# Moving the tiles that TensorE reads to multiples of 256 bytes in a hybrid encoder layer

## The chip, the core and the metric

The kernel runs on one core of a Trainium2 chip. The metric is the device time of one execution in microseconds, the median of several runs. An SBUF address is meant per partition: a tile of 128 x 512 float32 takes 2,048 bytes in each of 128 partitions.

## The reference, cut to what matters

One encoder layer is applied with the same weights to two inputs, a prompt of 1,024 tokens and a sample of 512, both 1,024 wide, in float32.

```python
proj = rmsnorm(x, g_attn) @ w_in                 # 1024 x 5120: qa ka va qb kb vb, two gates
a = dilated_mixture(qa, ka, va) @ w_a_out        # 12 heads in 3 dilation groups
bo = window_gqa(qb, kb, vb, sink) @ w_b_out      # 8 heads, window of +-128, sink per head
g_a, g_b = split(sigmoid(gates + b_gate))
x = x + (g_a * a + g_b * bo) @ w_o
u = dwconv(rmsnorm(x, g_ffn) @ w_up)             # 1024 x 5632, width 3
x = x + (gelu(u_gate) * u_val) @ w_down          # 2816 x 1024
y = rmsnorm(x, g_final)
```

## The kernel before, in words

**Precision.** Every float32 operand of a product is split into two float32r tiles, a rounded `hi` and the rest `lo`, and a product is three matmuls: hi by hi, hi by lo, lo by hi (`mm3`, lines 144 to 149; `accumulate`, lines 793 to 805; `product`, line 932; `down`, lines 1056 to 1058). Weights are loaded by SP's queue into `raw`, rounded by ScalarE (line 138) and their rests are taken by GpSimd or VectorE (line 141).

**The order of the work.** First the sample, then the prompt: norm and transposes, attention, merge (gates, branch projections, w_o), feed-forward. The sample's feed-forward (`ffn`) multiplies directly. In its loop the prompt's norm is done too (`norm_in`, line 206). The prompt's up-projection (`up_strassen`) makes seven products m1 to m7 per block of 128 columns in place of eight, each of 12 matmuls; m1, m2, m5, m6 have the moving operands b11, b21, t1, t2, which lie in the pool hp1024, and m4, m3, m7 have t4, b22, t3, which lie in hc1024. The order in the loop is m1, m2, m5, m6, then m4 and m3 of the block before, then m7. The prompt's `down` follows.

**Matmuls.** 7,944 matmuls have 512 moving columns. In `mm3` and `product` the moving operand is the activation and the stationary one (the weights of the array) a 128 x 128 piece of a weight tile; in the accumulations of lines 801 to 803 the moving operand is the weight tile and the stationary one the activation. The value projections (lines 289 to 291) have 256 moving columns of weights and the activations as stationary operand.

**Memory.** A pool is a stack entry: pools opened one after another lie one behind the other, some from the lower end of SBUF upwards (the default side), some from the upper end downwards. The sample's own pools lie at the lower end, except its inputs `xin` and small norm tiles `nsm`; the prompt's lie at the upper end, except the tiles of the Strassen weights and sums and hc. A tile's size is rounded up to 32 bytes. All tiles that matmuls read, but for two of the setup, are multiples of 512 bytes. So a pool of short tiles (`sm`, `ms`, `fsm`, `nsm`: 16 to 768 bytes each) shifts each pool that is opened behind it. A pool's first tile takes the lowest buffer, the next ones the others from the highest down. When a pool is closed, the next pool that is opened takes its place, and the first write of a tile waits for the last reader of the tiles that lay there (`reuse_waits="tile"`). The framework orders each engine's instructions itself, by priority and a model of times.

The lower end begins at byte 16,512, the upper end of the last pool is 229,344. At the lower end come the constants: `ident` (512 bytes), `eps`, `warm`, `sink`, `nsink` (32 each after rounding), `vecs` (832), so the next pool begins at 17,984, which is 70 x 256 + 64; 229,344 is 895 x 256 + 224. With the sizes of the pools this gives each pool's start modulo 256, which all its 512-byte pieces share:

| pools | start modulo 256 |
|---|---|
| raw, split (weights hi, lo); hp512 (the sample's activations); ptp512, qk512, vg512 (its attention); abp512, mg512, wop512 (its merge); wdp512 (its w_down); hc1024, rw1024 (Strassen operands and split weights, down's operands) | 64 |
| gvp512 (the sample's gated values, behind fsm512) | 192 |
| hp1024, ptp1024, qk1024, vg1024, abp1024, mg1024 (the prompt's) | 224 |
| xin512, xin1024 (behind nsm) | 96 |
| ident | 128 |

The pool mg1024 lies at 57,312 to 73,696, hp1024 at 163,808 to 229,344.

**The seam at the sample's feed-forward.** The last step of the merge (`accumulate`, lines 793 to 805) adds the blocks 6 and 7 of `merged` into x, token tile by token tile. Their operands lie in mg512, at 149,056 to 165,440: `mhi` in four buffers of 2,048 bytes, then `mlo`. Block 4 has the lowest buffer of mhi, block 7 the second, block 6 the third, block 5 the highest. The gate tiles mtp512 lie at 128,576 to 149,056. Then `begin_prompt` opens hp1024 and calls `begin_norm` (lines 1107 to 1109), which opens nsm1024 (4,224 bytes) and xin1024 (four tiles of 4,096 bytes, 143,200 to 159,584) from the upper end downwards; the sample's feed-forward takes its normalized tiles `xn` from xin1024. `rstd` (line 171 on) squares the x tiles on ScalarE into xn (line 175), takes a square root (line 176), and VectorE scales (line 190) before TensorE transposes (line 198).

**Constants.** `sink` is loaded by SP's queue (line 1139), negated on VectorE into `nsink` (line 1141) and used in `window_rows` (line 541) and, negated, in `window_unit`.

## Time and profile before

| | |
|---|---|
| median of 3 runs | 2,314.33 us (2,311.37 to 2,317.36) |
| profiled execution | 2,317.28 us, span 2,315.4 us |
| mean granted TensorE clock | 0.982 of full |
| TensorE busy | 2,207.3 us, 95% of the span |
| VectorE, ScalarE, GpSimd busy | 53%, 44%, 23% |
| DMA | 240.80 MB, mean 104 GB/s |

The span runs from the first to the last instruction of the program. A busy engine is one that has an instruction in flight; matmuls overlap, so the duration of one is longer than the distance to the next, and a stage in which TensorE is busy throughout can still become shorter if that distance does. L147 is line 147 of the kernel; `psg<-hhi,whi` names the tile that is written and the tiles that are read.

### The profile page before, as it was taken

What the parts mean: (1) busy time and instruction counts of PE and PEld (TensorE: products, weight loads), DVE (VectorE), ACT (ScalarE), POOL (GpSimd) and SP (SyncE); (2) the same over time, 40 slices, a digit from 0 to 9 for tenths busy, and PEclk for the clock granted to TensorE, in tenths of its full rate; (3) what the DMA queues carried; (4) which work ended last, traced back from release to release, by engine and by line L of the source; (5) the groups of instructions that cost most, each with busy time, mean ns of one, the idle gap of its engine ahead of it and who ended that gap; (6) DMA issues with size and microseconds to landing.
All of it is one profiled execution on the core that took longest, in us unless ns stands there. A gap on an engine that the chain in (4) does not pass through costs nothing.

```text
span 2315.4 us, 28400 instructions
## 1 busy us (share of the span) xinstructions
PE 2207.3 (95%) x10626; PEld 1820.2 (79%) x10626; DVE 1238.4 (53%) x2143; ACT 1015.8 (44%) x1868; POOL 542.3 (23%) x322
## 2 busy tenths in 40 slices
PE   6999899899999999999999999996899999999997
PEld 5887677688878788988787688885788888888886
DVE  4547533544465446465685534325867776763534
ACT  4646532533444336555575221114544444443332
POOL 2211254333333411100000432223332222200000
PEclk9999999999999999999999899998899999999999
DMA  5453442333333322413114711113122222254543
GB/s 159 141 167 113 146 153 85 110 94 98 100 124 94 100 78 60 129 58 110 51 49 120 217 44 50 44 35 118 37 83 86 79 81 82 78 200 150 173 152 112
DMA packets 247838, 240.80 MB, mean 104 GB/s; under 512 B 19792, under 2 KB 204832, under 8 KB 247700
## 3 DMA queue, kind: packets, MB, share of 16 engines
q1 hardware_dynamic: 247416, 238.89, 33.1%
q8 instruction: 83, 1.36, 0.2%
q14 instruction: 55, 0.45, 0.1%
q10 hardware_dynamic: 284, 0.11, 0.0%
HBM read 202.46 MB, written 42.79 MB: 106 GB/s over the span
## 4 chain that ended last, share of the span: by engine, by line
PE 78%; DVE 4%; ACT 2%; issue 2%; POOL 2%; DMA 1%; SPq 0%; DVEq 0%; ACTq 0%; POOLq 0%
PE psuA L932 10%; PE psuC L932 5%; PE pacc L803 4%; PE pacc L802 4%; PE pacc L801 4%; PE psg L147 3%; PE psg L149 3%; PE psg L148 3%; PE pacc L1058 3%; PE pacc L1056 3%; PE pacc L1057 3%; PE psu L147 3%; PE psu L149 3%; PE psu L148 3%; PE psuB L932 2%
## 5 line engine op out<-in xcount | busy, mean ns | idle before, releaser
L141 POOL TENSOR_TENSOR wlo<-raw,whi 128x1024 fp32r<-128x1024 f32 (+1 forms) x120 | 282.5, 2360 | 883.9 <-ACT whi L138 675.0
L138 ACT CAST whi<-raw 128x1024 fp32r<-128x1024 f32 (+1 forms) x178 | 182.1, 1029 | 385.8 <-PE pacc L803 137.1
L805 DVE TENSOR_TENSOR xacc<-xacc,pacc 128x512 f32<-128x512 f32 x236 | 160.5, 688 | 144.7 <-PE pacc L803 142.7
L147 PE MATMUL psg<-hhi,whi 128*128 128x512 f32 x384 | 152.0, 396 | 1.2 <-ACT frow L505 1.2
L141 DVE TENSOR_TENSOR wlo<-raw,whi 128x1024 fp32r<-128x1024 f32 (+1 forms) x58 | 74.4, 1282 | 147.2 <-ACT whi L138 124.6
L148 PE MATMUL psg<-hlo,whi 128*128 128x512 f32 x384 | 151.9, 395 | 0.0
L149 PE MATMUL psg<-hhi,wlo 128*128 128x512 f32 x384 | 151.7, 395 | 0.0
L147 PE MATMUL psu<-hhi,whi 128*128 128x512 f32 x352 | 137.5, 391 | 0.0
L149 PE MATMUL psu<-hhi,wlo 128*128 128x512 f32 x352 | 137.4, 391 | 0.0
L148 PE MATMUL psu<-hlo,whi 128*128 128x512 f32 x352 | 137.1, 390 | 0.0
L1057 PE MATMUL pacc<-rlo,rhi 128*128 128x512 f32 x352 | 137.1, 389 | 0.0
L1058 PE MATMUL pacc<-rhi,rlo 128*128 128x512 f32 x352 | 137.0, 389 | 0.0
L1056 PE MATMUL pacc<-rhi 128*128 128x512 f32 x352 | 137.0, 389 | 0.0
L939 DVE TENSOR_TENSOR rlo<-wraw,rhi 128x512 fp32r<-128x512 f32 x88 | 57.3, 689 | 133.2 <-ACT rhi L938 133.2
L968 POOL TENSOR_TENSOR rsum<-rraw 128x512 f32<-128x512 f32 x44 | 65.7, 1493 | 267.2 <-DMA rraw<-in_w_up_dram 251.2
L938 ACT CAST rhi<-wraw 128x512 fp32r<-128x512 f32 x88 | 50.5, 618 | 147.3 <-PE pacc L1058 137.9
L783 DVE TENSOR_TENSOR sg<-sg,psa 128x512 f32<-128x512 f32 x48 | 33.0, 687 | 153.2 <-PE psa L149 119.0
L938 ACT CAST rhi<-rsum 128x512 fp32r<-128x512 f32 x88 | 54.4, 622 | 117.7 <-PE psuC L932 71.2
L147 PE MATMUL psq<-hhi,whi 128*128 128x512 f32 x240 | 100.3, 418 | 1.1 <-DVE vb L341 0.6
L148 PE MATMUL psq<-hlo,whi 128*128 128x512 f32 x240 | 96.7, 403 | 0.0
L149 PE MATMUL psq<-hhi,wlo 128*128 128x512 f32 x240 | 96.2, 401 | 0.0
L399 DVE TENSOR_TENSOR ptlo<-pst,pthi 128x512 fp32r<-128x512 f32 (+1 forms) x128 | 82.7, 654 | 14.9 <-ACT pthi L398 13.4
(249 smaller groups left out, 6119.7 us busy)
## 6 DMA issues: line engine op xcount, KB each, us to landing
raw<-in_w_in_dram SPq DMA_DIRECT2D x80, 512.0 KB
raw<-in_w_up_dram SPq DMA_DIRECT2D x44, 512.0 KB
rraw<-in_w_up_dram SPq DMA_DIRECT2D x44, 512.0 KB
wraw<-in_w_down_dram SPq DMA_DIRECT2D x44, 512.0 KB
raw<-in_w_down_dram SPq DMA_DIRECT2D x22, 512.0 KB
gv<-y SPq DMA_DIRECT2D x22, 512.0 KB
graw<-gv SPq DMA_DIRECT2D x44, 256.0 KB
raw<-in_w_o_dram SPq DMA_DIRECT2D x16, 512.0 KB
```

The costliest lines, as they stand in the source:

```text
L138: nc.scalar.copy(out=hi[:, :n], in_=raw[:, :n])
L141: eng.tensor_tensor(out=lo[:, :n], in0=raw[:, :n], in1=hi[:, :n].bitcast(F32), op=ALU.subtract)
L147: mm(out, whi, r[0], start=start, stop=False)
L148: mm(out, whi, r[1], start=False, stop=False)
L149: mm(out, wlo, r[0], start=False, stop=stop)
L801: mm(p, a, whi[:, cols], start=i == 0, stop=False)
L805: nc.vector.tensor_tensor(out=x, in0=x, in1=p, op=ALU.add)
L932: mm(out, a[:, cols], b, start=start and j == 0 and n == 0, stop=j == 3 and n == 2, skip_group_check=True)
L938: nc.scalar.copy(out=hi, in_=src)
L1056: mm(p, a, whi, start=k == 0, stop=False)
L1057: mm(p, a, wlo, start=False, stop=False)
L1058: mm(p, b, whi, start=False, stop=k == FT - 1)
```

## The change

It changes where tiles lie, by three means. The short constants go into one tile `vecs` of 224 columns (896 bytes), and the separate `sink` goes: it is loaded into `nsink`, negated there, and `window_rows` subtracts it where it added `sink`. The constants then end at 17,920, which is 70 x 256. At the upper end a pool `top` with one tile of 224 bytes is opened first and never used, so the next pool ends at 229,120, which is 895 x 256. And pools of short tiles are opened behind those with tiles that TensorE reads: sm and ms last in `attention`, fsm behind gvp in `ffn`, nsm behind xin in `begin_norm`. All pools of the table then start at a multiple of 256, except `ident`, which stays where it is (at 128).

```diff
 window_rows
-                                in1=self.c["sink"][:, h].unsqueeze(1).to_broadcast([P, NT, 4]), op=ALU.add)
+                                in1=self.c["nsink"][:, h].unsqueeze(1).to_broadcast([P, NT, 4]), op=ALU.subtract)
 attention
         self.op = pool("ost", 4 if wide else 2)
-        self.sm = pool("sm", 2)
-        self.ms = pool("ms", 1)
         self.ptp = pool("ptp", 5 if wide else 4)
...
         self.vs = pool("vs", 2 if wide else 1)
+        self.sm = pool("sm", 2)
+        self.ms = pool("ms", 1)
 ffn
+        gvp = pool("gvp", 3)
         sm = pool("fsm", 2)
-        gvp = pool("gvp", 3)
 begin_norm
+        self.xin = self.pool(ctx, "xin", 4, side=side)
         self.nsm = self.pool(ctx, "nsm", 2, side=side)
-        self.xin = self.pool(ctx, "xin", 4, side=side)
 hybrid_encoder_kernel
-    c["eps"] = const.tile([P, 1], F32, name="eps")
+    vecs = const.tile([P, 224], F32, name="vecs")
+    top = ctx.enter_context(tc.tile_pool(name="top", bufs=1, side="right" if nc.default_side == "left" else "left"))
+    top.tile([P, 56], F32, name="top")
+    c["eps"], c["nsink"] = vecs[:, 208:209], vecs[:, 210:218]
     nc.gpsimd.memset(c["eps"], EPS)
-    warm = const.tile([P, 1], F32, name="warm")
-    nc.scalar.activation(out=warm, in_=c["eps"], func=AF.Sqrt)
+    nc.scalar.activation(out=vecs[:, 209:210], in_=c["eps"], func=AF.Sqrt)
     c["g_final"] = g_final
-    c["sink"] = const.tile([P, 8], F32, name="sink")
-    nc.sync.dma_start(c["sink"], bass.AP(tensor=sink.tensor, offset=sink.offset, ap=[[0, P], [1, 8]]))
-    c["nsink"] = const.tile([P, 8], F32, name="nsink")
-    nc.vector.tensor_scalar(out=c["nsink"], in0=c["sink"], scalar1=-1.0, scalar2=None, op0=ALU.mult)
-    vecs = const.tile([P, 208], F32, name="vecs")
+    nc.sync.dma_start(c["nsink"], bass.AP(tensor=sink.tensor, offset=sink.offset, ap=[[0, P], [1, 8]]))
+    nc.vector.tensor_scalar(out=c["nsink"], in0=c["nsink"], scalar1=-1.0, scalar2=None, op0=ALU.mult)
...
-        nc.vector.tensor_copy(out=vecs, in_=pv[:, 0:208])
+        nc.vector.tensor_copy(out=vecs[:, 0:208], in_=pv[:, 0:208])
```

## Rows read from the trace of the kernel before

**Rows 1.** The page, part 1: busy time, share of the span and instructions by engine.
```profile
PE 2207.3 (95%) x10626; PEld 1820.2 (79%) x10626; DVE 1238.4 (53%) x2143; ACT 1015.8 (44%) x1868; POOL 542.3 (23%) x322
```
**Rows 2.** Windows: the prompt's attention, merge, up- and down-projection; length, busy by engine, PEclk.
```profile
core 0: us, PE busy (x) PEld busy (x) DVE busy (x) ACT busy (x) POOL busy (x), PEclk, DMA share, GB/s
820.00:1248.00 428.00, 417.02 (x2539) 360.58 (x2538) 257.02 (x644) 252.31 (x614) 39.93 (x24) 0.99 0.24 75
1248.00:1597.00 349.00, 343.11 (x1443) 272.95 (x1441) 131.43 (x178) 76.58 (x103) 102.69 (x58) 0.98 0.32 90
1627.00:2066.00 439.00, 432.49 (x1858) 350.63 (x1857) 313.82 (x352) 219.69 (x328) 121.41 (x83) 0.99 0.26 86
2066.00:2303.00 237.00, 237.00 (x1047) 196.09 (x1046) 101.58 (x175) 82.30 (x147) 0.00 (x0) 1.00 0.45 151
```
**Rows 3.** Groups by line and shape, TensorE: busy us, mean ns of one, idle before.
```profile
L1056 PE MATMUL pacc<-rhi 128*128 128x512 f32 x352 | 137.0, 389 | 0.0
...
L932 PE MATMUL psuA<-b11hi,rhi 128*128 128x512 f32 x88 | 34.8, 396 | 0.0
...
L932 PE MATMUL psuA<-t3hi,rhi 128*128 128x512 f32 x88 | 34.3, 390 | 0.0
```
**Rows 4.** Timeline, TensorE: first and 48th matmul of a sample gate block (start us, us).
```profile
377.57 0.39 PE L147 MATMUL psg<-hhi,whi 128*128 128x512 f32 x1
...
388.22 0.39 PE L149 MATMUL psg<-hhi,wlo 128*128 128x512 f32 x1
```
**Rows 5.** Timeline, TensorE: first and 48th matmul of a prompt gate block.
```profile
1397.48 0.39 PE L147 MATMUL psg<-hhi,whi 128*128 128x512 f32 x1
...
1408.48 0.40 PE L149 MATMUL psg<-hhi,wlo 128*128 128x512 f32 x1
```
**Rows 6.** Timeline, TensorE, one Strassen round: first matmuls of m1, m4, m3, next m1.
```profile
1825.27 0.40 PE L932 MATMUL psuA<-b11hi,rhi 128*128 128x512 f32 x1
...
1836.51 0.39 PE L932 MATMUL psuA<-t4hi,rhi 128*128 128x512 f32 x1
...
1839.27 0.39 PE L932 MATMUL psuC<-b22hi,rhi 128*128 128x512 f32 x1
...
1844.71 0.40 PE L932 MATMUL psuA<-b11hi,rhi 128*128 128x512 f32 x1
```
**Rows 7.** Timeline, TensorE: first and 48th matmul, sample's down, then prompt's w_o accumulation.
```profile
638.66 0.40 PE L801 MATMUL pacc<-whi,ghi 128*128 128x512 f32 x1
...
649.58 0.40 PE L803 MATMUL pacc<-whi,glo 128*128 128x512 f32 x1
...
1428.39 0.40 PE L801 MATMUL pacc<-whi,mhi 128*128 128x512 f32 x1
...
1439.37 0.39 PE L803 MATMUL pacc<-whi,mlo 128*128 128x512 f32 x1
```
**Rows 8.** Timeline, TensorE, value projections: sample (42 matmuls), prompt (192), first and last.
```profile
92.57 0.28 PE L289 MATMUL psv<-whi,hhi 128*128 128x256 f32 x1
...
97.49 0.28 PE L291 MATMUL psv<-whi,hlo 128*128 128x256 f32 x1
...
820.70 0.39 PE L289 MATMUL psv<-whi,hhi 128*128 128x256 f32 x1
...
843.72 0.28 PE L291 MATMUL psv<-whi,hlo 128*128 128x256 f32 x1
```
**Rows 9.** Tile vb: sample 234 to 252, prompt 1140 to 1248 us; duration ns min/median/max.
```profile
L409 PE MATMUL pso<-pthi,vb x15: 276/282/389, 235.0 to 250.6; 128*128 128x256 f32 x15
...
L409 PE MATMUL pso<-pthi,vb x88: 278/282/415, 1140.9 to 1246.9; 128*128 128x256 f32 x88
```
**Rows 10.** Waits of TensorE, whole span: us in total, times, longest us.
```profile
PE psuA L932 <- ACT ug L979: 6.5, 1, 6.5
```
**Rows 11.** Timeline, ScalarE, start of the sample's feed-forward: squares of three x tiles.
```profile
422.86 1.06 ACT L175 ACTIVATE xn<-xacc 128x1024 f32<-128x1024 f32 x1 [0.51 <-DVE xacc L805]
...
429.52 1.06 ACT L175 ACTIVATE xn<-xacc 128x1024 f32<-128x1024 f32 x1 [5.51 <-PE pacc L803]
...
430.58 1.04 ACT L175 ACTIVATE xn<-xacc 128x1024 f32<-128x1024 f32 x1
```
**Rows 12.** Timeline, ScalarE, start of the kernel: the square root of eps.
```profile
2.65 0.20 ACT L1136 ACTIVATE warm<-eps 128x1 f32<-128x1 f32 x1
```

## The prediction

> **What bounds the kernel now.** I read the page first [rows 1]: TensorE is busy for 95% of the span, the next engine, VectorE, for 53%. The table by stage [rows 2] shows TensorE busy for 417 of 428 us in the prompt's attention, 343 of 349 in its merge, 432 of 439 in its up-projection and all of 237 in its down-projection. So in all of them the time is the number of matmuls times the distance from one start to the next, and the question is what sets that distance. 7,944 of the 10,622 matmuls (counted in the program; this count and those below are of its loops) have 512 moving columns.

> The view by line and shape [rows 3] shows that equal matmuls are not equally long: 389 ns for one of the down-projection and 390 for product m7 (t3), but 396 for product m1 (b11), with a granted clock of 0.99 and 1.00 of full over these stages [rows 2]. A matmul of 512 columns overlaps the next, so the pace has to come from starts. In the sample's gates the 48 matmuls of one column block and branch pair start between 377.57 and 388.22 [rows 4]: 47 steps in 10.65 us, 226.6 ns. The prompt's gates take 11.00 us for the same 47 steps [rows 5], 234.0 ns. In the Strassen loop [rows 6], the 48 matmuls of m1, m2, m5 and m6 take 11.24 us, 234.2 ns; the 24 of m3 and m7 take 5.44 us, 226.7 ns. Same shapes, same loop, same clock.

> What differs is where the operands lie. Call the start modulo 256 bytes the phase (the table of pools gives it). The sample's gates have both operands at 64, m3 and m7 too. The prompt's gates and m1, m2, m5, m6 have the moving operand at 224 and the weights at 64. The two other mixed kinds are slow too [rows 7]: the prompt's w_o accumulation (moving 64, weights 224) takes 47 steps in 10.98 us, 233.6 ns; the sample's down accumulation (moving 64, weights 192) 47 in 10.92, 232.3 ns. High addresses are not the cause: the weights of the w_o accumulation lie at 57 to 73 KB.

> Is it the phase itself, or that the two differ? Short matmuls speak. With 256 columns the sample's value projection (64 and 64) makes 41 steps in 4.92 us, 120.0 ns, and the prompt's (64 and 224) 191 steps in 23.02, 120.5 [rows 8]: no penalty there. The window values with 256 columns have both operands at 64 in the sample and both at 224 in the prompt; their median duration is 282 ns in both [rows 9]. So 224 as such costs nothing that shows; at 512 columns a difference between the two does. That is the reading that I take: operands of one phase run at 226.6 ns.

> **The change, part by part.** I make the sum against the profiled execution: 2,317.28 us, of which the span is 2,315.4; it stands 2.95 us over the median of 2,314.33.

> The move to phase 0. All operands of matmuls of 512 columns then have one phase; the nearest rows are those at 64 and 64, so I take 226.6 ns. The bounds are no gain (234 stays) and a further step of the same size, as a rival below.
> - 2,976 matmuls with moving operand 224 and weights 64 (864 projections of queries, keys and window values, 768 gates, 288 of the branch outputs, 1,056 Strassen): 7.5 ns each [rows 4 to 6], 22.3 us.
> - 384 of the prompt's w_o accumulation: 7.0 ns, 2.7 us.
> - 528 of the sample's down accumulation: 5.7 ns, 3.0 us.
> - m4 has one phase already, yet 12 steps take 2.76 us after m6 (1836.51 to 1839.27), 230 ns [rows 6]; a slow product seems to leave something behind it. 264 such matmuls by 3.4 ns: 0.9 us.

> Together 28.9 us. The first three are 3,888 matmuls; the other 4,056 stand at 64 and 64 and gain nothing. Transposes (identity still at 128) and the 256-column matmuls are left as they are, by rows 8 and 9.

> What gives time back. In the prompt's attention, where 6.5 of those us lie (864 by 7.5 ns), TensorE stands idle for 11 us, mostly in waits for other engines' copies [rows 2]; an earlier TensorE waits longer for these. I take a third, 2.2 us, between 0 and 6.5. Product m6 of the first round waits 6.5 us, behind VectorE's and ScalarE's work on the quadrants [rows 10]; the 36 matmuls before it gain 0.3 us and lose it there.

> The order of pools changes which old tile lies under a new one, and a first write waits for the old tile's last reader. I went through the seams. One new wait stands out, at the sample's feed-forward. The first xn tile lies today at 143,200 to 147,296, over gate tiles that are long free, and ScalarE squares x there at 422.86, seven us ahead of the second, which waits for TensorE's last accumulation [rows 11]. With xin above nsm that buffer starts at 163,584 - 16,384 = 147,200 and ends at 151,296; mg's tile of block 7 starts at 151,040 (64 lower than now). So the first square too waits for the last accumulation, and two squares, 1.06 us from start to start, stand before the transposes in place of one: 1.1 us. Behind it on ScalarE are the third square and both square roots. The scheduler may order them anew, so 0 to 2 us. For the other seams (252, 820, 1248 us) the new neighbours are tiles read long before, or the same ones; I cost them at nothing, since the first writes there come tens of us after the last reads; without that cover a seam would cost what this one does.

> The constants. The same number of instructions stays: one memset, one square root, one broadcast load, one negation, four subtractions in place of additions. They now write into one tile, but into separate columns, so no queue gains a wait; should the load of sink, the first on SP's queue and ahead of the x loads there, wait for the square root, SP would start when that ends, at 2.85 us [rows 12], so at most 2.9 us later. I take 0.

> Sum: 28.9 - 2.2 - 0.3 - 1.1 = 25.3 us; 2,317.28 - 25.3 = 2,292.0 in the profiled execution's terms, 2,289.0 as a median. With the terms' bounds (give-back 0 to 11.7: attention 6.5, m6 0.3, seam 2, start 2.9) and the 3 us by which the runs differ from their median, 2,282 to 2,300.

> **Rivals.** *Phase is not what sets the pace.* Then all stays and the seam adds 1.1: 2,315. For it: tile sizes and stages differ too, between fast and slow groups. Against it: m7 and m1 are the same line, shape and loop, with weights from the same pool [rows 6]. 0.08. [...]

> *The pace improves, the stages don't follow.* VectorE and ScalarE, at 314 and 220 of 439 us in the up-projection [rows 2], become late next, and half of 25 is given back: 2,302. Against it: m3 and m7 run at 226.7 with nothing waiting. 0.08.

> *Phase 0 is better than any equal phase.* Then all 7,944 matmuls gain, say one more step of 7 ns: 55.6 us on top, 2,233. [...] Against: equal phases of 64 and 224 do not differ in rows 9. 0.10. [...]

> *Two operands at phase 0 collide.* All reads then begin on the same boundary, and the 4,056 matmuls that are fast now go to 234 ns, while the others stay: 4,056 by 7.5 ns and the seam, 31.5 us, 2,346. It decides from a pace of 230.1 ns on (226.6 plus 28.0 us over 7,944), above which the change loses. Against: the fast ones share a phase already. 0.10.

> **How the numbers follow.** The forecast has 0.64, alone 2,282 to 2,300. With the second rival and the first the chance is 0.80, so the range is 2,280 to 2,317; the last two rivals are left out. 0.3% (about what a measurement of this kernel can tell from no change) is 6.9 us: faster is below 2,307.4, slower above 2,321.3. Faster: 0.64, 0.10 and 0.07 of the second rival, 0.81; same 0.09; slower 0.10.

> **What would show it.** Right: 47 steps of the prompt's gates in 10.65 us; the seven products of a Strassen round, 19.44 us from m1 to m1 [rows 6], in 19.04; durations of 389 in place of 396; the first xn square beside the second, after the last accumulation. Wrong: gates at 11.00 us as before; any 512-column run well under 226 ns or, in the sample, over 230; or the pace there but PE's idle time up by more than 12 us.

## The result and the profile after

The changed kernel takes 2,291.72 us (median of 4 runs, 2,290.15 to 2,294.84) against 2,315.04 us for the kernel before in the same job (4 runs, 2,311.37 to 2,317.36). The ratio is 0.990, with a 95% interval from 0.9887 to 0.9913. Timed again later, beside another kernel, it took 2,293.68 us (5 runs, 2,290.89 to 2,295.38), ratio 0.9898 (0.9878 to 0.9919). The profiled execution took 2,290.39 us with a span of 2,288.6, 26.8 less than before, and a mean granted clock of 0.984. By the medians of that job the gain is 23.3 us.

Part 1 of the page of the changed kernel, which answers to [rows 1]:

```profile
PE 2178.7 (95%) x10626; PEld 1813.7 (79%) x10626; DVE 1242.4 (54%) x2143; ACT 1015.5 (44%) x1868; POOL 542.8 (24%) x322
```

The same number of instructions, TensorE still busy for 95% of a shorter span, the other engines busy within 4 us of their old times. So the time came out of TensorE's own work. The timeline of TensorE shows where. The changed kernel, first and 48th matmul of a block of the prompt's gates, the block of [rows 5]:

```profile
1385.94 0.39 PE L147 MATMUL psg<-hhi,whi 128*128 128x512 f32 x1
...
1396.59 0.39 PE L149 MATMUL psg<-hhi,wlo 128*128 128x512 f32 x1
```

47 steps in 10.65 us, 226.6 ns each, where they took 11.00 us; the granted clock is 1.00 in both blocks. The same view for the first matmuls of m1, m4, m3 and the next m1 in the Strassen round of [rows 6]:

```profile
1803.34 0.39 PE L932 MATMUL psuA<-b11hi,rhi 128*128 128x512 f32 x1
...
1814.22 0.39 PE L932 MATMUL psuA<-t4hi,rhi 128*128 128x512 f32 x1
...
1816.94 0.39 PE L932 MATMUL psuC<-b22hi,rhi 128*128 128x512 f32 x1
...
1822.38 0.39 PE L932 MATMUL psuA<-b11hi,rhi 128*128 128x512 f32 x1
```

The 48 steps of m1, m2, m5 and m6 take 10.88 us (before 11.24), the 12 of m4 take 2.72 (before 2.76), the 24 of m3 and m7 take 5.44, as before. The round is 19.04 us long in place of 19.44. The sample's down accumulation and the prompt's w_o accumulation, as in [rows 7]:

```profile
636.30 0.39 PE L801 MATMUL pacc<-whi,ghi 128*128 128x512 f32 x1
...
646.96 0.39 PE L803 MATMUL pacc<-whi,glo 128*128 128x512 f32 x1
...
1415.86 0.39 PE L801 MATMUL pacc<-whi,mhi 128*128 128x512 f32 x1
...
1426.51 0.39 PE L803 MATMUL pacc<-whi,mlo 128*128 128x512 f32 x1
```

Both are at 47 steps in 10.65 or 10.66 us. In the sample's gates, which were fast before [rows 4], nothing moves: a block now runs from 374.19 to 384.84.

What that does to the stages is seen when each is cut at the first matmul of its own and of the next. Windows of the prompt's attention, merge and up-projection and of the sample's feed-forward, first of the kernel before (columns as in [rows 2]):

```profile
820.70:1248.08 427.38, 416.40 (x2537) 360.40 (x2537) 256.36 (x643) 252.06 (x614) 39.93 (x24) 0.99 0.24 76
1248.08:1597.39 349.31, 343.42 (x1444) 273.15 (x1441) 131.39 (x178) 76.53 (x102) 102.69 (x58) 0.98 0.32 91
1626.96:2058.62 431.66, 425.15 (x1827) 344.82 (x1826) 306.57 (x345) 216.11 (x323) 121.43 (x84) 0.99 0.25 81
435.29:820.70 385.41, 379.04 (x1681) 308.55 (x1681) 198.73 (x293) 157.29 (x215) 131.17 (x65) 0.99 0.32 100
```

and of the changed kernel:

```profile
817.75:1240.56 422.81, 410.90 (x2537) 357.50 (x2537) 256.09 (x643) 252.38 (x614) 39.96 (x24) 1.00 0.25 76
1240.56:1579.77 339.21, 332.99 (x1443) 272.15 (x1441) 131.66 (x178) 76.57 (x102) 102.22 (x58) 0.98 0.32 93
1608.23:2031.82 423.59, 415.96 (x1827) 343.44 (x1826) 311.90 (x345) 215.42 (x323) 123.26 (x84) 0.99 0.26 83
434.19:817.75 383.56, 377.09 (x1680) 308.97 (x1680) 198.65 (x294) 157.60 (x215) 131.15 (x65) 0.99 0.33 101
```

The attention is 4.6 us shorter, the merge 10.1, the up-projection 8.1 and the sample's feed-forward 1.8. TensorE's idle time (length less PE busy) grows only from 11.0 to 11.9, from 5.9 to 6.2 and from 6.5 to 7.6 us in the first three.

The seam at the sample's feed-forward changed as [rows 11] let one foresee. ScalarE's timeline of the changed kernel, the squares of three x tiles (the short reads of the sums between them left out), and TensorE's last accumulation and first transposes there:

```profile
427.32 1.06 ACT L175 ACTIVATE xn<-xacc 128x1024 f32<-128x1024 f32 x1 [6.22 <-PE pacc L802]
...
428.38 1.04 ACT L175 ACTIVATE xn<-xacc 128x1024 f32<-128x1024 f32 x1
...
429.41 1.04 ACT L175 ACTIVATE xn<-xacc 128x1024 f32<-128x1024 f32 x1
```

```profile
427.07 0.39 PE L803 MATMUL pacc<-whi,mlo 128*128 128x512 f32 x1
...
434.19 1.14 PE L198 MATMUL pst<-ident,xn 128*128 128x128 f32 x4 [6.73 <-DVE xn L190]
```

The first square stands beside the second, behind the last accumulation, and TensorE's wait for xn is 6.73 us. Among its waits it was 5.85 before (the experiments e7 and e9 show the pair of them again), and product m6 waits 7.6 us for ScalarE where it waited 6.5 [rows 10].

### The profile page after: what moved, and what is told of

Its sections match the earlier page's. It is cut to its first block, busy times and chain, and to the rows that moved or that the text cites. A ratio compares the mean times of both kernels' runs of the same rounds, so it can differ in the third digit from the quotient of the medians.

```text
span 2288.6 us, 28398 instructions
## 1 busy us (share of the span) xinstructions
PE 2178.7 (95%) x10626; PEld 1813.7 (79%) x10626; DVE 1242.4 (54%) x2143; ACT 1015.5 (44%) x1868; POOL 542.8 (24%) x322
## 4 chain that ended last, share of the span: by engine, by line
PE 77%; DVE 5%; ACT 2%; POOL 2%; DMA 2%; issue 2%; SPq 0%; DVEq 0%; ACTq 0%; POOLq 0%
PE psuA L932 10%; PE psuC L932 5%; PE pacc L803 4%; PE pacc L802 3%; PE pacc L801 3%; PE pacc L1058 3%; PE pacc L1056 3%; PE pacc L1057 3%; PE psu L149 3%; PE psu L148 3%; PE psu L147 3%; PE psg L148 3%; PE psg L149 3%; PE psg L147 3%; PE psuB L932 2%; PE pso L409 2%
## 5 line engine op out<-in xcount | busy, mean ns | idle before, releaser
L968 POOL TENSOR_TENSOR rsum<-rraw 128x512 f32<-128x512 f32 x44 | 59.5, 1352 | 263.1 <-DMA rraw<-in_w_up_dram 246.2
```

## Experiments

The theory after the result was that of the prediction: a matmul of 512 columns is long where its two operands start at different phases (start modulo 256). The rivals were that the size of a pool's alignment counts (multiples of 256 or 64 are good as such), that one side alone counts, and that the order of the pools brings the gain. Most edits below change only where tiles lie, by the widths of the unused tile `top` and of `vecs`, or by the order of pools; e6 adds two pools, and e10 widens tiles and takes one buffer away. Kernels with a single run are read by their paces, since seven runs of the kernel before in one job lay between 2,312.1 and 2,322.7 us.

**e1_top64: the kernel before with one tile more.** A pool with an unused tile of 160 bytes at the upper end brings the prompt's pools to 64, where the weights lie already. No constant is packed, no pool reordered.

```diff
     vecs = const.tile([P, 208], F32, name="vecs")
+    top = ctx.enter_context(tc.tile_pool(name="top", bufs=1, side="right" ...))
+    top.tile([P, 40], F32, name="top")
```

> The kernel before with one edit: a tile of 160 bytes at the upper end, so that the prompt's pools start at 64 modulo 256 like the weights; gvp512 stays at 192, nothing else moves, no pool order changes. Theory (what costs time is a difference of phase between the moving operand and the weights): the prompt's gates take 10.65 us for 47 steps, a Strassen round 19.04 us, the prompt's w_o accumulation 226.6 ns per step, and only the sample's down accumulation stays at about 232; the time is that of the changed kernel plus 1 to 3 us, about 2,294. Rival (a start at a multiple of 256 is what counts): at 64 the prompt's gates stay at 234 ns and the time at about 2,314.

Measured: 2,295.60 us (4 runs, 2,293.44 to 2,296.67), ratio 0.990 (0.9886 to 0.9915). TensorE's timeline of this kernel, the prompt's gates and the sample's down accumulation:

```profile
1391.93 0.39 PE L147 MATMUL psg<-hhi,whi 128*128 128x512 f32 x1
...
1402.58 0.39 PE L149 MATMUL psg<-hhi,wlo 128*128 128x512 f32 x1
```

```profile
638.57 0.39 PE L801 MATMUL pacc<-whi,ghi 128*128 128x512 f32 x1
...
649.48 0.40 PE L803 MATMUL pacc<-whi,glo 128*128 128x512 f32 x1
```

The gates run at 226.6 ns with both operands at 64. The sample's down, left at 64 and 192, runs at 232.1 ns (232.3 before). So nearly the whole gain of the change can be had from 160 unused bytes, and a multiple of 256 isn't needed.

**e2_both32: everything at 32.** The changed kernel with all pools shifted by 32 bytes.

```diff
-    vecs = const.tile([P, 224], F32, name="vecs")
+    vecs = const.tile([P, 232], F32, name="vecs")
-    top.tile([P, 56], F32, name="top")
+    top.tile([P, 48], F32, name="top")
```

> The changed kernel with both ends moved by 32 bytes, so that all pools start at 32 modulo 256, a multiple of neither 64 nor 256. Theory (difference of phase): every run of 512 columns stays at 226.6 ns, the time is that of the changed kernel, about 2,291. Rival (multiples of 256, or of 64, count): all 7,944 matmuls of 512 columns go to 234 ns or more, 2,291 + 7,944 x 7.5 ns = about 2,350.

Measured: 2,295.97 us (4 runs, 2,289.78 to 2,298.39), ratio 0.9901 (0.9876 to 0.9926). The gates, again 47 steps in 10.65 us:

```profile
1389.06 0.39 PE L147 MATMUL psg<-hhi,whi 128*128 128x512 f32 x1
...
1399.71 0.39 PE L149 MATMUL psg<-hhi,wlo 128*128 128x512 f32 x1
```

Phases 0, 32 and 64 give one and the same pace, 226.6 ns, when both operands have them. The alignment itself is worth nothing here. Nor need the starts agree modulo 512. The sizes of these pools are multiples of 512, and in the changed kernel the lower ones begin at 70 x 256 and the upper ones end at 895 x 256, so the prompt's activations and their weights differ by an odd multiple of 256, and the pace is 226.6 ns all the same; a difference of 128 is slow (233.4 ns in e3, below).

**e8_lower_only: half of the change.** The changed kernel without `top`: weights and sample at 0, the prompt at 224.

```diff
-    top = ctx.enter_context(tc.tile_pool(name="top", ...))
-    top.tile([P, 56], F32, name="top")
```

> The changed kernel without the 224 bytes at the upper end: weights and the sample's tiles at 0, the prompt's at 224. Theory (difference of phase): the prompt's gates at 234 ns per step and its w_o accumulation at 233, as before; only the sample's down accumulation gains (226.6); about 2,291 + 25 = 2,314. Rival (each operand off a multiple of 256 costs by itself): weights at 0 help, the prompt's gates come to some 230 ns, about 2,302.

Measured: 2,315.21 us in one run. The gates take 10.97 us for 47 steps, 233.4 ns:

```profile
1397.66 0.40 PE L147 MATMUL psg<-hhi,whi 128*128 128x512 f32 x1
...
1408.63 0.40 PE L149 MATMUL psg<-hhi,wlo 128*128 128x512 f32 x1
```

Weights at a multiple of 256 help nothing while the activations lie at 224.

**e3_upper128 and e4_upper64: other differences.** The changed kernel with a smaller `top`, so that the prompt's pools lie at 128 or at 64 while weights and sample stay at 0.

```diff
-    top.tile([P, 56], F32, name="top")
+    top.tile([P, 24], F32, name="top")        # e3; 40 in e4
```

> The changed kernel with the prompt's pools at 128 instead of 0, the weights at 0. Theory (any difference of phase costs the same step): the prompt's gates, Strassen's m1, m2, m5, m6 and the w_o accumulation at 232 to 235 ns, as at a difference of 160; about 2,291 + 26 = 2,317. Rival (only a start off a multiple of 64 or 128 costs): 226.6 ns, about 2,291.

> The changed kernel with the prompt's pools at 64 instead of 0, the weights at 0. Theory (any difference of phase below 256 costs): the prompt's gates and m1, m2, m5, m6 at 232 to 235 ns per step, time about 2,308 to 2,317. Rival (only differences that are no multiple of 64 or 128, or only those of 128 and of 32, cost): the gates at 226.6 ns, about 2,291.

Measured, one run each: e3 2,308.82 us, e4 2,301.75 us. In e3 the gates run at 233.4 ns (1392.24 to 1403.21 us for 47 steps), as the theory had it, but the time is 8 us under the expected 2,317. That sum had given back the whole gain of the change, although the sample's down accumulation stays fast here and the slow steps are about 1 ns shorter than at a difference of 160; the rest of a single run isn't explained. In e4 five of the sixteen blocks of the prompt's gates run at 233.3 ns and the others at about 229, so one and the same difference can give two paces. The time was lower than expected, and the timeline says in part why. The 48 steps of m1, m2, m5 and m6, moving operand at 64 and weights at 0, and then the first and last of the prompt's 192 value projections with 256 columns, where the weights move (0) and the activations (64) are stationary:

```profile
1812.64 0.40 PE L932 MATMUL psuA<-b11hi,rhi 128*128 128x512 f32 x1
...
1823.64 0.40 PE L932 MATMUL psuA<-t4hi,rhi 128*128 128x512 f32 x1
```

```profile
820.59 0.39 PE L289 MATMUL psv<-whi,hhi 128*128 128x256 f32 x1
...
842.36 0.28 PE L291 MATMUL psv<-whi,hlo 128*128 128x256 f32 x1
```

The Strassen products take 11.00 us, 229.2 ns, between the two paces known so far. The value projections take 114.0 ns per step (191 in 21.77 us) where [rows 8] have 120.5. So 64 is mostly not as dear as the other differences, and with 256 columns a difference can even help. The latter was tried by itself in e10.

**e6_lo_apart: whose weights count?** In the kernel before, the load of the weights for the second matmul of m4 starts together with the first matmul, at 1836.51 us (rows 6), and takes 0.19 us where that matmul takes 0.39:

```profile
1836.51 0.19 PEld L932 LDWEIGHTS psuA<-t4lo,rhi 128*128 128x128 f32 x1
```

So either a matmul's own weights or the next one's could collide with its moving operand. Here only the `lo` weights get another phase (0), by a pool of their own; the `hi` weights and the activations have 128. The Strassen weights and hc, which open in another place, stay at 0, so m1, m2, m5 and m6 have a difference of 128 in this kernel and run at 233 ns; the reading is of the sample.

```diff
-    top.tile([P, 56], F32, name="top")
+    top.tile([P, 24], F32, name="top")
+    rest = w_ctx.enter_context(tc.tile_pool(name="rest", bufs=3, reuse_waits="tile"))
+    pad = w_ctx.enter_context(tc.tile_pool(name="pad", bufs=1))
+    pad.tile([P, 32], F32, name="pad")
...
-            return (raws if tag == "raw" else split).tile(*a, tag=tag, **kw)
+            return {"raw": raws, "whi": split, "wlo": rest}[tag].tile(*a, tag=tag, **kw)
```

> The changed kernel with the tiles of the weights' rests (wlo) in a pool of their own at 0, the weights' hi tiles, the activations of sample and prompt, and all else at 128. Of three matmuls of a product step, in the order hi weights by hi, hi weights by lo, rest weights by hi, only the third has operands of unequal phase. Theory a (a matmul's own moving operand against its own weights): the step that begins with the third matmul is long, the other two 226.6 ns. Theory b (a matmul's moving operand against the weights of the next, which are loaded while it runs): the step that begins with the second matmul is long, the others 226.6 ns. Theory c (an unequal pair disturbs what follows for several matmuls): two or all three are long. In each the mean of the sample's gates lies between 226.6 and 229.3 (a third of 8 ns more) for a and b, up to 234 for c.

Measured: 2,310.25 us in one run. The order in `mm3` is line 147 (whi), 148 (whi), 149 (wlo), then 147 again. The view by line and shape of the sample's up-projection, this kernel and then the changed one:

```profile
L149 PE MATMUL psu<-hhi,wlo 128*128 128x512 f32 x352 | 139.9, 398 | 0.0
L148 PE MATMUL psu<-hlo,whi 128*128 128x512 f32 x352 | 139.5, 397 | 0.0
L147 PE MATMUL psu<-hhi,whi 128*128 128x512 f32 x352 | 137.6, 391 | 0.0
```

```profile
L147 PE MATMUL psu<-hhi,whi 128*128 128x512 f32 x352 | 137.3, 391 | 0.0
L149 PE MATMUL psu<-hhi,wlo 128*128 128x512 f32 x352 | 137.2, 390 | 0.0
L148 PE MATMUL psu<-hlo,whi 128*128 128x512 f32 x352 | 137.0, 390 | 0.0
```

Line 149, whose own weights differ, is 8 ns longer, and line 148, whose own weights agree but whose successor's differ, is 7 ns longer. Line 147, where both agree, is as short as before, though the weights after next differ. From start to start it is 226.9 ns after line 147 (469 steps), 232.4 after 148 (472) and 234.1 after 149 (456), 231.1 in the mean, more than theories a and b allow. Neither of them held alone; that two steps are long is theory c, but the third step isn't, right behind an unequal pair.

That the next matmul's weights count is shown, and the kernel before shows it, too: the last matmul of the sample's up-projection ahead of each down accumulation has equal operands and unequal weights behind it, and its step is 232.4 ns long (mean of 11; 227.5 in the changed kernel). That a matmul's own weights count isn't shown: line 149 also stands behind a long step, and slow steps can lengthen equal ones behind them. Product m4 of the kernel before shows that. Its operands and the weights behind them all lie at 64, but it follows m6, which is slow. Its tenth matmul in the round of [rows 6]:

```profile
1838.59 0.39 PE L932 MATMUL psuA<-t4hi,rhi 128*128 128x512 f32 x1
```

The nine steps ahead of it take 2.08 us, 231.1 ns each, and the three from it to m3 0.68 us, 226.7 ns. Behind the sample's slow down accumulation it is the same: the first four steps of the up-projection take 230.8 ns in the mean of ten places, and 226.7 in the changed kernel.

**e7_nsm_first and e9_order_only: the order of the pools.** e7 is the changed kernel with `begin_norm` in its old order; e9 is the kernel before with the new orders alone (in `attention`, `ffn` and `begin_norm`, as in the diff of the change).

```diff
 begin_norm                                     # e7
-        self.xin = self.pool(ctx, "xin", 4, side=side)
         self.nsm = self.pool(ctx, "nsm", 2, side=side)
+        self.xin = self.pool(ctx, "xin", 4, side=side)
```

> The changed kernel with begin_norm's old order (nsm opened before xin), so that xin lies at 128; no matmul of 512 columns reads it. Theory: the first square of the sample's feed-forward no longer waits for the last accumulation, the gap between the last accumulation and the first transpose of xn goes from 7.1 us back to 6.2, all paces stay at 226.7, and the time is that of the changed kernel less about 1 us, 2,291, which a median of few runs cannot tell from it. Rival (xin's phase counts, too): the transposes of xin and xn slow down from 109 ns and the time rises by over 1 us.

> The kernel before with the new order of pools alone (sm and ms last, fsm behind gvp, nsm behind xin), the constants and the upper end as they were: weights at 64, prompt at 224, gvp at 64. Theory: the sample's down accumulation at 226.7 ns, the prompt's gates at 234; 2,315 - 3 + 1 = about 2,313. Rival (the order of pools, by other waits, brings part of the gain): about 2,305.

Measured: e7 2,292.91 us (4 runs, 2,291.72 to 2,296.66), ratio 0.9901 (0.9879 to 0.9924); e9 2,318.47 us in one run, 5 above the expectation and among the kernel before's own runs. TensorE's last accumulation and first transposes at the seam, in e7 and then in e9:

```profile
430.69 0.39 PE L803 MATMUL pacc<-whi,mlo 128*128 128x512 f32 x1
...
436.93 1.35 PE L198 MATMUL pst<-ident,xn 128*128 128x128 f32 x5 [5.85 <-DVE xn L190]
```

```profile
429.36 0.39 PE L803 MATMUL pacc<-whi,mlo 128*128 128x512 f32 x1
...
436.48 0.90 PE L198 MATMUL pst<-ident,xn 128*128 128x128 f32 x3 [6.73 <-DVE xn L190]
```

From start to start it is 6.24 us with the old order and 7.12 with the new, with and without the rest of the change. That the order costs 0.88 us here is shown. It is too little to be seen in the medians: e7 isn't faster than the changed kernel. The transposes of xin and xn keep their median pace of 109 ns, so xin's phase didn't count. In e9 the gates keep their slow pace (1398.34 to 1409.34 us for 47 steps, 234.0 ns) and the order alone brings no gain. Only the sample's down accumulation, which the order brings from 192 to the weights' 64, comes down, to 226.6 ns (638.55 to 649.20).

**e10_v192: the value weights at 192.** In e4 the value projections were faster with moving weights 192 above the activations (0 less 64, modulo 256). Here the changed kernel's value weights are put at column 48 (192 bytes) of tiles made 64 columns wider, and nothing else that TensorE reads leaves its phase. To make room, the norm's scratch tile gets one buffer in place of two.

```diff
-    def wload(self, srcs, ncols, pool=None):
+    def wload(self, srcs, ncols, pool=None, off=0):
-        hi = (pool or self.wp).tile([P, 1024], F32R, tag="whi", name="whi")
+        hi = (pool or self.wp).tile([P, 1024 if pool else 1088], F32R, tag="whi", name="whi")[:, off:off + 1024]
...
-            ws.append(self.wload([...VA + g * 256:VA + g * 256 + 256]], 256))
+            ws.append(self.wload([...VA + g * 256:VA + g * 256 + 256]], 256, off=48))
...
+        self.jk = self.pool(ctx, "jk", 1, side=side)
```

> The changed kernel with the split weights of the value projections (256 moving columns) 192 bytes into their tiles, so that the moving operand lies at 192 and the activations at 0; the weight tiles are 256 bytes longer, and the squares' junk tile of the norm is one in place of two, to make room. Theory (at 256 columns this difference is faster than none, as the run with the prompt's pools at 64 showed: 113 and 114 ns in place of 120): the 864 value steps take 113 to 114 ns, 864 x 6.4 ns = 5.5 us less where TensorE sets the pace, some 3 to 5 us, about 2,288. Rival (that was an effect of the place, not of the difference; or the stage waits for others anyway): 120 ns, or the time unchanged at 2,292.

> The changed kernel itself, beside the run before it on the same chip, for the comparison. Both theories: about 2,292.

Measured, side by side: e10 2,287.36 us (4 runs, 2,281.22 to 2,289.35), ratio to the kernel before 0.9867 (0.9844 to 0.989); the changed kernel again (e11) 2,293.68, ratio 0.9898 (0.9878 to 0.9919). The prompt's value projections in the changed kernel and then in e10:

```profile
817.75 0.38 PE L289 MATMUL psv<-whi,hhi 128*128 128x256 f32 x1
...
840.76 0.28 PE L291 MATMUL psv<-whi,hlo 128*128 128x256 f32 x1
```

```profile
815.31 0.39 PE L289 MATMUL psv<-whi,hhi 128*128 128x256 f32 x1
...
837.08 0.28 PE L291 MATMUL psv<-whi,hlo 128*128 128x256 f32 x1
```

191 steps take 23.01 us (120.5 ns) at equal phase and 21.77 us (114.0 ns) at a difference of 192, so the theory's pace is shown in the prompt. In the sample the steps without a wait went from 120.4 to 116.3 ns, not to 114. The prompt's attention, from its first value projection to the first matmul of its gates, is 3.2 us shorter than in e11 (419.4 against 422.6), and its value steps, waits included, 3.1 (66.9 against 70.0).

The medians differ by 6.3 us, and not all of that is the pace. The sample's value steps take 37.9 us against 40.7 in e11, but 2.2 of that difference are one wait for the first `lo` weights at 16 us, which in e10 doesn't stand between value steps. And the longer weight tiles push the sample's pools up by 6 x 256 bytes, so the first xn tile no longer lies over a tile that the last accumulation reads, and the seam is back at 6.24 us (7.12 in e11):

```profile
423.98 0.39 PE L803 MATMUL pacc<-whi,mlo 128*128 128x512 f32 x1
...
430.22 1.56 PE L198 MATMUL pst<-ident,xn 128*128 128x128 f32 x6 [5.84 <-DVE xn L190]
```

So some 4 us are the value steps' and 0.9 the seam's; the rest has no owner. The two intervals overlap, but each of the four runs of e10 is shorter than each of the five of e11.

## Why the prediction was right

The forecast was 2,289.0 us (alone 2,282 to 2,300), and 2,291.7 was measured; the profiled execution came out at 2,290.4, against 2,292.0. The gain was put at 25.3 us; it is 23.3 by the medians and 26.9 between the profiled executions. Its steps:

- **The pace at equal phase.** Right in the gates, the Strassen products, the branch outputs and the accumulations: 226.6 to 227.1 ns where 226.6 was taken. The reason held too. It is the difference that costs, not one phase as such: 64 is fast beside 64 (226.6 ns, e1) and slow beside 0 (229 to 233.3, e4), and 0 is fast beside 0 (226.6) and slow beside 224 (233.4, e8). Two operands at 224 with 512 columns were not run. By starts in the trace the classes gained, with the forecast in brackets, 5.8 us in the prompt's gates (768 by 7.5 ns is 5.8), 7.4 in m1, m2, m5 and m6, of which m6's longer wait is taken off already (7.9), 2.5 in the w_o accumulation (2.7), 1.8 in the branch outputs (2.2).
- **The sample's down accumulation.** Its pace came down as forecast, from 232.3 to 226.8 ns, but the class gained 1.7 us in place of 3.0, and the stage was 1.8 shorter. TensorE waits here for the gated values too, and part went to those waits (5.0 us before, 5.7 after). This term was too large.
- **m4 behind m6.** Forecast 0.9, measured 0.9 (264 steps, 60.7 us before and 59.8 after). "Something left behind" was right: the nine long steps of m4 (at e6) have equal phases throughout, so the unequal pairs of e6 don't account for them. What is carried over stays open.
- **The give-back in the prompt's attention.** Net 4.6 us were gained where 6.5 less 2.2 is 4.3. In the windows, TensorE's busy time fell by 5.5 and its idle time rose by 0.9, so both terms were about 1 us too large and cancelled: that the net came out is luck. The first was too large because the 864 projection steps went from 234.0 ns to 228.7 in the mean of those without a wait (227 in the median), not to 226.6.
- **The wait of m6.** Forecast 0.3 us more, measured 1.1 (6.5 to 7.6).
- **The seam.** Forecast 1.1 us, measured 0.88, by the mechanism that was named: the first square behind the last accumulation, undone in e7 and made alone in e9.
- **Constants and other seams.** Taken at nothing. The terms above leave some 3 us of the 26.8 without an owner: 2.0 ahead of the sample's gates, whose first matmul starts at 250.3 us in place of 252.3, and 1.1 in the transposes between merge and up-projection (28.5 us in place of 29.6). The change isn't shown to be their cause: in e11, the changed kernel once more, the sample's gates start at 253.2 us and the transposes take 28.8.
- **The value projections, "left as they are".** Their pace didn't change with this change (120.0 and 120.5 ns, as in [rows 8]), but rows 8 held the differences 0 and 96 only. That no difference matters with 256 columns would have been wrong: at 192 they were faster (114.0 ns in e4 and e10).

The rivals fell at one row each. That the phase isn't the cause: e1 moves one pool boundary and gets the gain. That the stages don't follow: the windows above. That phase 0 is better than other equal phases: e2 at 32 has the pace of the changed kernel at 0, 226.6 ns. That two operands at 0 collide: the sample's gates, now at 0 and 0, are at 226.6 ns as before.

## What to carry to other kernels

Where TensorE is busy throughout and still slower than the same shape elsewhere in the same kernel, compare the starts of its two operands modulo 256 bytes: here 512-column float32r matmuls lost 3 to 8 ns of 234 when these differed, and a pad of 160 bytes won back 1% of the time. What counted here is that they agree, with each other (226.6 ns with both at 0, 32 or 64) and with the weights that follow (232.4 ns where only those differed), not which address they have, so a pool of short tiles opened ahead of others can change the pace of what lies behind it: the sample's down accumulation took 232.3 ns with gvp512 behind fsm512 and 226.6 with that order turned (e9). A slow stretch also slowed the first matmuls behind it, nine of m4 in the round of [rows 6] (231.1 ns, then 226.7). A new order of pools also says which old tile a first write waits for; read that from the addresses, as at this seam, where it cost 0.88 us.

## What the runs showed of the hardware

| difference | ns per step | seen in |
|---|---|---|
| 0 (both at 0, 32 or 64) | 226.6 to 226.8 | changed kernel, e2, e1 |
| 32 | 233.2 | e8, w_o accumulation |
| 64 | about 229; 233.3 in five of sixteen blocks of gates | e4 |
| 96 | 233.6 | before, w_o accumulation |
| 128 | 232.3 (64 and 192); 232.4 to 233.4 | before, sample's down; e3, gates |
| 160 | 234.0 to 234.4 | before, gates and Strassen |
| 192 | 233.3 | e4, w_o accumulation |
| 224 | 233.4 | e8, gates |

The table gives means; step by step the pace is uneven. Averaged over the 22 rounds, the steps of product m2 alternate between 237.5 and 229.2 ns at a difference of 128 (e3), go 231.5, 226.3, 228.9 and again at 64 (e4), and repeat after seven steps, between 231.1 and 237.5, at 160 (before).

Unexpected was that with 256 columns the sign turns, in the first 192 value projections of the prompt: 120.0 to 120.5 ns at the differences 0 and 96, 119.2 at 128 (e3), 118.4 at 32 (e8), 114.0 at 192 (e4 and e10). Why, the runs don't say.

Also open is the rest of the step. At equal phase 512 columns take 226.6 ns and 256 take 120.0, so 256 more columns are 106.6 ns, 0.416 ns each. If every column takes that long, an estimate from these two paces, some 13.4 ns of each step come on top at either width; what they are, no run shows. In e6 a step was 232.4 ns long where only the next matmul's weights differed; how they come to count, no run shows either.
